# Three moves in the transfer order of a fused attention kernel: q's low parts, the gate load, the attention store

## The chip, the cores and the metric

The kernel runs on one core of a Trainium2 chip. The metric is the device time of one execution in microseconds (us). The engines are named as in the profile: PE (TensorE), DVE (VectorE), ACT (ScalarE), POOL (GpSimd) and SP (SyncE, which here only issues DMAs; ACT issues some too).

## The reference, cut to what matters

A decoder layer on a sequence of 1024 rows of 1024 values, all float32. One normalised input is projected to nine blocks; a convolution branch and an attention branch use them, and a gated merge joins the two. The change lies in the attention branch. It has 24 heads of 64 values, in three groups of eight heads; group g attends in a band at stride 1, 4 or 16. The three groups are then merged by the weights of their softmaxes, and the result is gated by silu of z_att:

```
m = jnp.max(scores, axis=-1)
p = jnp.exp(scores - m[..., None])
den = jnp.sum(p, axis=-1)
o = jnp.einsum('bdhnqk,bdhnke->bdhnqe', p, vb) / den[..., None]
...
m_all = jnp.maximum(jnp.maximum(maxes[0], maxes[1]), maxes[2])
wts = [d_g * jnp.exp(m_g - m_all) for m_g, d_g in zip(maxes, dens)]
w_sum = wts[0] + wts[1] + wts[2]
att = (wts[0][..., None] * outs[0] + wts[1][..., None] * outs[1]
       + wts[2][..., None] * outs[2]) / w_sum[..., None]
y_att = (att * jax.nn.silu(z_att)) @ w_att_out[layer]
```

## The kernel before, in words

**Precision.** Matrices of the projections are split into a high and a low fp32r part, and every product is three matmuls: high by high (L73), low by high (L74), high by low (L75). Of q, too, a high and a low part are kept, so that the scores of one tile are q's high part by k (L843) and its low part by k (L844).

**The attention phase** runs from about 640 to 1082 us as one loop over slots (L970 to L1016). The 24 heads are taken as 12 pairs of heads n, numbered so that n = 3j + g: j is one of four blocks of two heads per group, g the group. A pair has 8 slots, a slot has one unit of work of each kind on PE, in an order that is written out by hand:

1. twelve matmuls L73 to L75 into PSUM tile `d`: the projection of a coming pair's q and k (part 0 and part 1, each in two halves of 512 rows), and after the last pair of the gates;
2. the scores of this slot (L843, L844) into `s`;
3. the transposes (L860) of the exponentials of two slots earlier into `t`, copied to `pt` by DVE (L865) or ACT (L863);
4. the values (L875) of three slots earlier into `o`;
5. what the dictionary `beside` holds for this slot.

DVE masks the scores and takes their maxima (L847, L850), ACT takes the exponentials (L852). The orders of DVE, ACT, POOL and SP are set by a scheduler from the order of the code and its own estimates; each engine then runs its list strictly in that order.

**From projection to scores.** ACT and DVE write each projected part to a tile `kqp` (two buffers; L720, L721). From there small DMAs on SP's queue (`move`, L785, two of 128 KB for each move, eight per part for k and q together) carry k and q to the tiles that PE reads. q's low half goes its own way: `load_low(n)` issues the four `ql` DMAs of pair n in slot 4 of the pair before, together with the load of v (`vt`). DMAs that SP and ACT issue share eight completion semaphores that are handed out in turn, so a DMA is not issued before the one that came eight places earlier in the program has landed; that may be a store of ACT's (`oscr`, L684; `ascr`, L730) which itself still waits for its data.

**The combination.** When the three groups of a block j have stored their outputs to `oscr[j]`, `combine(j, half)` merges them, once for each half of the rows. It is a generator of six steps, and `FIRST` and `SECOND` name the slots, counted from the one in which the last group is done, in which the steps of the two halves are emitted:

- step 1: the load `rd` (L885, 792 KB, one buffer for both halves);
- step 2: maxima (`ma`, L897, L898), differences (L902), an exponential on ACT (L903), and the load `at` of the gate (L905, one buffer for both halves);
- step 3: the small sums and their reciprocal (L908 to L913);
- step 4: two of the three wide products (L917);
- step 5: the third product (L917), two sums (L920, L922), which leave `pr`;
- step 6: four transposes of `pr` on PE (L926) into `t`, the product with the gate (L927), the store to `atscr` (L929).

With n the pair in which block j ends, that slot is 8n + 10. For j = 0, 1, 2 the second half's step 6 falls in the first slot of pairs 5, 8 and 11, that is slots 40, 64 and 88. Slot 40 begins its scores at 844.91 us in the profile, slot 64 at 947.05, slot 88 at 1049.41.

Of the kernel before, what the change touches and what calls it, by code (L numbers as in the profile page):

```python
# [8 lines left out]
F32 = mybir.dt.float32  # L9
# [7 lines left out]
P = 128  # L17
# [22 lines left out]
def layer(ctx: ExitStack, tc: tile.TileContext, a, out):  # L40
    nc = tc.nc
# [10 lines left out]
    def sbuf_pool(name, **kw):  # L52
        return tc.tile_pool(name=name, bufs=1, reuse_waits="tile", **kw)

    def split(hi, lo, raw, lo_eng=None):

        nc.scalar.activation(hi, raw, AF.Copy)  # L57
        (lo_eng or nc.vector).tensor_sub(lo, raw, hi.bitcast(F32))  # L58
# [44 lines left out]
    zascr = [dram.tile([P, S], F32, name=f"zascr{j}") for j in range(4)]  # L103
    atscr = [dram.tile([P, S], F32, name=f"atscr{j}") for j in range(3)]
# [66 lines left out]
    with sbuf_pool("start") as st, tc.manual_schedule(  # L171
# [15 lines left out]
        def load_v(kp):  # L187
            raw = wpool.tile([P, 1024], F32, name="wraw", tag="wraw", bufs=3)
            for c in (slice(0, 512), slice(512, 1024)) if kp == 0 else (slice(0, 1024),):
                nc.sync.dma_start(raw[:, c], a["w_v"][0, kp][:, c])  # L190
            v_raw.append(raw)
# [148 lines left out]
        for kt in range(KT):  # L340
# [10 lines left out]
            for i, (wh, wl) in enumerate(u_w):  # L351
                for half in range(2):
                    s = slice(half * 512, half * 512 + 512)
# [292 lines left out]
    ap_ = c_ctx.enter_context(sbuf_pool("att"))  # L646

    def pair_tile(n, name, dt=F32R):
        return stk.tile([P, 2, S], dt, name=name, tag=f"s{n}")
# [13 lines left out]
    def v_load(vt, g, j):  # L663
        c0 = g * 512 + j * P
        cols = vscr[:, c0:c0 + P]
        if g == 0:
            nc.sync.dma_start(vt, cols.rearrange("(t p) c -> p t c", p=P))
        elif g == 1:
            v = cols.rearrange("(b p r) c -> r p b c", b=2, r=4)
            for r in range(4):  # L670
                nc.sync.dma_start(vt[:, 2 * r:2 * r + 2], v[r])
        else:
            v = cols.rearrange("(i t s) c -> s i t c", t=8, s=2)
            for s in range(2):
                nc.sync.dma_start(vt[64 * s:64 * s + 64], v[s])
# [105 lines left out]
    def move(dst, row, n, part, i, which):  # L781

        for h in range(2):
            src = parts_of[n, part][64 * i + 32 * h:64 * i + 32 * h + 32, which]
            nc.sync.dma_start(dst[row + 32 * part:row + 32 * part + 32, h].bitcast(F32), src.bitcast(F32))  # L785
# [11 lines left out]
    def load_low(n):  # L797

        for part in range(2):
            move(q_low[n % 2], 0, n, part, 1, 1)  # L800
        v2[n] = stk.tile([P, 8, P], F32, name="vt", tag="vt", bufs=2)
        v_load(v2[n], order[n][1], order[n][0])
        if order[n][1] == 0:
            row = ap_.tile([P, 4, P], F32, name="row", tag="pr")
            for i in range(2):
                nc.sync.dma_start(row[:, i], bscr[i:i + 1, order[n][0] * P:(order[n][0] + 1) * P].to_broadcast([P, P]))
            late.append(add_row(v2[n], row))

    def add_row(vt, row):
        nc.vector.tensor_add(row[:, 0], row[:, 0], row[:, 1])  # L810
        yield
        for t in (slice(0, 4), slice(4, 8)):
            nc.vector.tensor_add(vt[:, t], vt[:, t], row[:, 0].unsqueeze(1).to_broadcast([P, 4, P]))
            yield
# [67 lines left out]
    def o_load(j, half):  # L882
        s = slice(half * 512, half * 512 + 512)
        rd = ap_.tile([P, 4, 3, 2, 66], F32, name="rd", tag="rd", bufs=1)
        nc.sync.dma_start(rd.rearrange("p t g h c -> p t (g h c)"),  # L885
                          oscr[j][s].rearrange("(t p) g c -> p t (g c)", p=P))
        return rd

    def combine(j, half):


        s = slice(half * 512, half * 512 + 512)
        rd = o_load(j, half)
        yield
        m, den = rd[:, :, :, :, 65], rd[:, :, :, :, 64]
        ma = ap_.tile([P, 4, 2], F32, name="ma")
        nc.vector.tensor_max(ma, m[:, :, 0], m[:, :, 1])  # L897
        nc.vector.tensor_max(ma, ma, m[:, :, 2])  # L898
        w = ap_.tile([P, 3, 4, 2], F32, name="w")
        wd = ap_.tile([P, 3, 4, 2], F32, name="wd")  # L900
        for g in range(3):
            nc.vector.tensor_sub(w[:, g], m[:, :, g], ma)  # L902
        nc.scalar.activation(w, w, AF.Exp, scale=SCALE)  # L903
        at = ap_.tile([P, 512], F32, name="at")
        nc.sync.dma_start(at, zascr[j][:, s])  # L905
        yield
        for g in range(3):
            nc.vector.tensor_mul(wd[:, g], w[:, g], den[:, :, g])  # L908
        nc.vector.tensor_add(wd[:, 0], wd[:, 0], wd[:, 1])
        nc.vector.tensor_add(wd[:, 0], wd[:, 0], wd[:, 2])  # L910
        nc.vector.reciprocal(wd[:, 1], wd[:, 0])
        for g in range(3):
            nc.vector.tensor_mul(w[:, g], w[:, g], wd[:, 1])  # L913
        yield
        o = [rd[:, :, g, :, 0:64] for g in range(3)]
        for g in range(3):
            nc.vector.tensor_mul(o[g], o[g], w[:, g].unsqueeze(3).to_broadcast([P, 4, 2, 64]))  # L917
            if g == 1:
                yield
        nc.vector.tensor_add(o[0], o[0], o[2])  # L920
        pr = ap_.tile([P, 4, 2, 64], F32, name="pr", tag="pr")
        nc.vector.tensor_add(pr, o[0], o[1])  # L922
        yield
        pt = psa.tile([P, 512], F32, name="t", tag="t")
        for t in range(4):
            nc.tensor.transpose(pt[:, t * P:(t + 1) * P], pr[:, t].rearrange("p h c -> p (h c)"), ident)  # L926
        nc.vector.tensor_mul(at, pt, at)  # L927
        if j < 3:
            nc.sync.dma_start(atscr[j][:, s], at)  # L929
        else:  # L930
            att_parts(3, s, at)
        yield

    ah, al = {}, {}

    def att_parts(j, s, raw):

        if j // 2 not in ah:
            ah[j // 2], al[j // 2] = pair_tile(j // 2, "ah"), pair_tile(2 + j // 2, "al")
        split(ah[j // 2][:, j % 2, s], al[j // 2][:, j % 2, s], raw)  # L940
# [23 lines left out]
    LEAD, TURN, VAL = 13, 2, 3  # L964
    stages = 8 * len(order)

    FIRST, SECOND = (2, 6, 6, 7, 7, 9), (8, 11, 11, 12, 12, 14)
    beside, heads = {}, {}

    with tc.manual_schedule(engines={nc.tensor.engine}):  # L970
        for slot_ in range(-LEAD, (2 * len(order) + KT) * 4 - LEAD):
            due, made[:] = made[:], []
            after = next(stream)
            for x in due:
                move_kq(*x)
                if x == (0, 1):
                    load_low(0)
            if 0 <= slot_ < stages:
                n, st_ = divmod(slot_, 8)
                if st_ == 0:  # L980
                    heads[n] = Attend(n)
                if st_ == 4 and n + 1 < len(order):
                    load_low(n + 1)
                heads[n].scores(st_)
            if TURN <= slot_ < stages + TURN:
                n, st_ = divmod(slot_ - TURN, 8)
                heads[n].turn(st_)
            if VAL <= slot_ < stages + VAL:
                n, st_ = divmod(slot_ - VAL, 8)
                heads[n].values(st_)  # L990
                if st_ == 7:
                    del heads[n]
                    j, g = order[n]
                    if g == 2:
                        for half, steps in enumerate((FIRST, SECOND)):
                            c = combine(j, half)
                            for x in steps:
                                beside.setdefault(slot_ + x, []).append(c)
            for c in beside.pop(slot_, ()):
                next(c)  # L1000
            for c in late:
                for x in (2, 2, 3):
                    beside.setdefault(slot_ + x, []).append(c)
            late[:] = []
            j = slot_ - stages - VAL
            if 0 <= j < 3:
                raw = load_raw(atscr[j])
                for half in range(2):
                    s = slice(half * 512, half * 512 + 512)
                    att_parts(j, s, raw[:, s])  # L1010
            if j in (4, 6, 8):
                w_out(0, j // 2 - 2)
            if j == 11:
                ahead = weights(a["w_ao"][0], 512)
            if after:
                after()  # L1016
        assert not beside and next(stream, None) is None
# [148 lines left out]
```

## Time and profile before

| | |
|---|---|
| time, median of 3 runs | 1278.72 us (1276.84 to 1278.82) |
| the profiled execution | 1277.71 us |
| its span in the trace | 1275.9 us |
| granted clock | 0.999 |
| PE busy | 1248.6 us, 98% |
| DVE, ACT, POOL busy | 890.5, 476.8, 94.7 us |

The profiled execution lies 1.0 us below the median and inside the three runs. Times in the text are microseconds from the start of its span. In rows of the timeline the columns are start, duration, engine, line, operation, tiles, number of instructions, and in brackets the idle time just before and what ended it. In rows of waits they are the total, the number of times and the longest. SPq and ACTq are the queues in which DMAs are issued; the duration there runs from the first issue of a row to the end of the last, waits between them included.

### The profile page before, as it was taken

To read this page: it belongs to the slowest core of one execution; us is meant where nothing else is said; L and a number is where in the kernel's file an instruction comes from. 1 tells how busy PE (TensorE), PEld (TensorE's weight loads), DVE (VectorE), ACT (ScalarE), POOL (GpSimd) and SP (SyncE) were. 2 spreads that over 40 slices of the span, in tenths; PEclk is the share of its full clock that TensorE was granted. 3 is DMA by queue.
4 is the path that set the end of the run, shared out by engine and by line. 5 is a ranking of instruction groups with operands and counts; after the bars stand their busy time and mean duration, and the time that the engine had idled before them with its cause. 6 is when DMAs were issued, how large, how long until landed. Compare 5 with 4: busy or idle time off the path is not lost.

```text
span 1275.9 us, 16604 instructions
## 1 busy us (share of the span) xinstructions
PE 1248.6 (98%) x6148; PEld 1050.6 (82%) x6148; DVE 890.5 (70%) x1576; ACT 476.8 (37%) x911; POOL 94.7 (7%) x78
## 2 busy tenths in 40 slices
PE   6999999999999999999999999999999989999997
PEld 4777888888888888888888888888888878888886
DVE  6777999999999986853345546766766563349544
ACT  4653212111222246720015545545444467534211
POOL 0000000000000000000042111111101012100000
PEclk9999999999999999999999999999999999999999
DMA  9522311211211112545666456576575566659221
GB/s 366 186 95 68 114 60 53 102 50 50 91 58 50 50 52 89 167 164 198 149 171 152 120 130 162 135 198 149 140 206 137 147 166 190 205 176 316 98 100 67
DMA packets 85526, 171.53 MB, mean 134 GB/s; under 512 B 11203, under 2 KB 41027, under 8 KB 85445
## 3 DMA queue, kind: packets, MB, share of 16 engines
q1 hardware_dynamic: 69024, 157.66, 41.9%
q10 hardware_dynamic: 16420, 12.80, 3.3%
q8 instruction: 49, 0.80, 0.3%
q14 instruction: 33, 0.26, 0.1%
HBM read 105.74 MB, written 33.23 MB: 109 GB/s over the span
## 4 chain that ended last, share of the span: by engine, by line
PE 91%; DVE 4%; DMA 2%; ACT 2%; issue 1%; SPq 0%; ACTq 0%; DVEq 0%
PE d L73 22%; PE d L75 22%; PE d L74 22%; PE o L875 4%; PE d L1070 2%; PE d L1069 2%; PE d L467 2%; PE d L466 2%; PE d L1071 2%; PE d L465 2%; PE t L860 2%; PE s L844 1%; PE s L843 1%; PE d L249 1%; PE d L247 1%; PE d L248 1%
## 5 line engine op out<-in xcount | busy, mean ns | idle before, releaser
L73 PE MATMUL d<-hh,whi 128*128 128x512 f32 x1072 | 427.5, 399 | 1.5 <-DVE gs L632 0.9
L74 PE MATMUL d<-hl,whi 128*128 128x512 f32 x1072 | 417.6, 390 | 1.9 <-DVE hl L347 1.9
L75 PE MATMUL d<-hh,wlo 128*128 128x512 f32 x1072 | 418.5, 390 | 0.0
L406 DVE SCALAR_TENSOR_TENSOR v<-u,cw,v 128x1024 f32<-128x1024 f32 x232 | 280.5, 1279 | 0.0
L75 PEld LDWEIGHTS d<-hh,wlo 128*128 128x128 f32 x1072 | 201.2, 188 | 43.9 <-POOL wlo L58 0.7
L74 PEld LDWEIGHTS d<-hl,whi 128*128 128x128 f32 x1072 | 201.7, 188 | 41.7 <-DVE hl L347 2.8
L73 PEld LDWEIGHTS d<-hh,whi 128*128 128x128 f32 x1072 | 201.6, 188 | 40.9 <-ACT whi L57 1.3
L57 ACT ACTIVATE whi<-wraw 128x512 fp32r<-128x512 f32 (+1 forms) x107 | 88.0, 834 | 269.6 <-PE d L74 236.1
L58 POOL TENSOR_TENSOR wlo<-wraw,whi 128x512 fp32r<-128x512 f32 (+1 forms) x56 | 84.8, 1529 | 658.0 <-ACT whi L57 556.2
L852 ACT ACTIVATE sb<-sb,nm 128x128 f32<-128x128 f32 (+1 forms) x192 | 85.0, 444 | 86.9 <-DVE nm L850 82.6
L847 DVE CUSTOM_DVE_ANT_0 sb<-s,mask 128x128 f32<-128x128 f32 (+1 forms) x192 | 59.7, 347 | 61.6 <-PE s L844 54.8
L875 PE MATMUL o<-vt,pt 128*128 128x64 f32 x560 | 73.5, 267 | 1.1 <-ACT pt L863 0.5
L875 PEld LDWEIGHTS o<-vt,pt 128*128 128x128 f32 x560 | 70.1, 192 | 2.1 <-DVE pt L865 1.3
L58 DVE TENSOR_TENSOR wlo<-wraw,whi 128x1024 fp32r<-128x1024 f32 (+1 forms) x51 | 57.9, 1137 | 15.6 <-ACT whi L57 15.0
L844 PE MATMUL s<-k,ql 128*128 128x128 f32 (+1 forms) x192 | 51.0, 279 | 3.2 <-DMA ql<-kqp 3.2
L465 PE MATMUL d<-vh,hh 128*128 128x512 f32 x128 | 49.8, 389 | 0.0
L466 PE MATMUL d<-vl,hh 128*128 128x512 f32 x128 | 49.8, 389 | 0.0
L467 PE MATMUL d<-vh,hl 128*128 128x512 f32 x128 | 49.8, 389 | 0.0
L73 PE MATMUL d<-uh,whi 128*128 128x512 f32 x128 | 49.8, 389 | 0.0
L74 PE MATMUL d<-ul,whi 128*128 128x512 f32 x128 | 49.8, 389 | 0.0
L75 PE MATMUL d<-uh,wlo 128*128 128x512 f32 x128 | 49.8, 389 | 0.0
L632 DVE TENSOR_TENSOR gs<-d,sgc 128x512 f32<-128x512 f32 x16 | 11.1, 691 | 54.9 <-PE d L75 48.8
(224 smaller groups left out, 1758.5 us busy)
## 6 DMA issues: line engine op xcount, KB each, us to landing
wraw<-in_w_t SPq DMA_DIRECT2D x67, 512.0 KB, 4.3
k<-kqp SPq DMA_DIRECT2D x96, 128.0 KB, 2.6
q<-kqp SPq DMA_DIRECT2D x96, 128.0 KB, 2.4
wa<-in_w_ada SPq DMA_DIRECT2D x16, 512.0 KB, 5.9
rd<-oscr SPq DMA_DIRECT2D x8, 792.0 KB, 5.1
ql<-kqp SPq DMA_DIRECT2D x48, 128.0 KB, 2.4
wraw<-in_w_v SPq DMA_DIRECT2D x11, 512.0 KB, 3.6
x<-in_xT SPq DMA_DIRECT2D x8, 512.0 KB, 10.2
```

What stands on the lines that cost most here:

```text
L57: nc.scalar.activation(hi, raw, AF.Copy)
L58: (lo_eng or nc.vector).tensor_sub(lo, raw, hi.bitcast(F32))
L73: nc.tensor.matmul(ps, lh, rh, start=start, stop=False)
L74: nc.tensor.matmul(ps, lh, rl, start=False, stop=False)
L75: nc.tensor.matmul(ps, ll, rh, start=False, stop=stop)
L406: nc.vector.scalar_tensor_tensor(d, u[:, k:k + S], cw[:, ct, k:k + 1], d, op0=mult, op1=add)
L465: nc.tensor.matmul(ps, hh[:, k, ts_], rh, start=k == 0, stop=False)
L466: nc.tensor.matmul(ps, hh[:, k, ts_], rl, start=False, stop=False)
L467: nc.tensor.matmul(ps, hl[:, k, ts_], rh, start=False, stop=k == KT - 1)
L844: nc.tensor.matmul(ps[:, c:c + w], self.ql[:, h, ts_], self.k2[:, h, ks], start=False, stop=True)
L852: nc.scalar.activation(sb[:, c:c + w], sb[:, c:c + w], AF.Exp, bias=nm[:, t - tp:t - tp + 1], scale=SCALE, accum_out=ov[:, t, h, 64:65])
L875: nc.tensor.matmul(self.po[:, t % 4, h], pt[:, c + i:c + i + P], self.vt[:, kb, r], start=i == 0, stop=i + P == w)
```

## The change

Three things are moved.

- `load_low(n)` is cut in two. The `ql` DMAs are issued as soon as part 1 of the pair has been moved, right behind its k and q; `load_v(n)`, the rest, stays in slot 4.
- The load of the gate `at` goes from step 2 to the end of step 5, and the store to `atscr` becomes a step 7, two slots behind step 6. For j = 3 there is no step 7.
- Steps 1 to 6 of the second half are one slot later: `SECOND` was (8, 11, 11, 12, 12, 14) and is (9, 12, 12, 13, 13, 15, 17).

```
+    def load_v(n):
         v2[n] = stk.tile([P, 8, P], F32, name="vt", tag="vt", bufs=2)
         v_load(v2[n], order[n][1], order[n][0])
...
         nc.scalar.activation(w, w, AF.Exp, scale=SCALE)
-        at = ap_.tile([P, 512], F32, name="at")
-        nc.sync.dma_start(at, zascr[j][:, s])
         yield
...
         nc.vector.tensor_add(pr, o[0], o[1])
+        at = ap_.tile([P, 512], F32, name="at")
+        nc.sync.dma_start(at, zascr[j][:, s])
         yield
...
         nc.vector.tensor_mul(at, pt, at)
-        if j < 3:
-            nc.sync.dma_start(atscr[j][:, s], at)
-        else:
+        if j == 3:
             att_parts(3, s, at)
+        yield
+        nc.sync.dma_start(atscr[j][:, s], at)
         yield
...
-    FIRST, SECOND = (2, 6, 6, 7, 7, 9), (8, 11, 11, 12, 12, 14)
+    FIRST, SECOND = (2, 6, 6, 7, 7, 9, 11), (9, 12, 12, 13, 13, 15, 17)
...
                 move_kq(*x)
-                if x == (0, 1):
-                    load_low(0)
+                if x[1]:
+                    load_low(x[0])
+                    if x[0] == 0:
+                        load_v(0)
...
                 if st_ == 4 and n + 1 < len(order):
-                    load_low(n + 1)
+                    load_v(n + 1)
...
-                            for x in steps:
+                            for x in steps[:6 if j == 3 else 7]:
```

Lines of the changed kernel are numbered two higher behind L800 (the load `rd` is L887, the scores' mask L849, the copy of `pt` L867), up to the gate load, which is now L924; the transposes of `pr` are L928, the product L929, the store L933. L922 is the same line in both.

SP's queue is the same in both up to the first combination. There, from the second half of block 0 on, it stood as follows before. `k` and `q` are the DMAs of pair 5, `rd` is the second half of block 0, `wraw` the weights of a later projection, `ql` and `vt` belong to pair 5.

```order
L785 DMA k_5884<-kqp 32x1024 x4
L785 DMA q_5885<-kqp 32x1024 x4
L885 DMA rd<-oscr_4279 128x4x396
L62 DMA wraw<-in_w_t 128x1024 x2
L785 DMA k_5884<-kqp 32x1024 x4
L785 DMA q_5885<-kqp 32x1024 x4
L929 DMA atscr_93<-at 128x512
L785 DMA ql<-kqp 32x1024 x4
L675 DMA vt<-vscr 64x8x128 x2
```

The same place of SP's queue in the changed kernel:

```order
L785 DMA k_5884<-kqp 32x1024 x4
L785 DMA q_5885<-kqp 32x1024 x4
L62 DMA wraw<-in_w_t 128x1024 x2
L785 DMA k_5884<-kqp 32x1024 x4
L785 DMA q_5885<-kqp 32x1024 x4
L785 DMA ql<-kqp 32x1024 x4
L887 DMA rd<-oscr_4279 128x4x396
L675 DMA vt<-vscr 64x8x128 x2
L933 DMA atscr_93<-at 128x512
```

`ql` has come ahead of the store `atscr`, and `rd` has gone behind two weight loads, four k and q transfers and `ql`. The same happens at blocks 1 and 2.

On DVE the second half of block 0 stood in slots 37 to 39 before: `ma` came at once behind L712 of slot 37. In slot 40 DVE's list before read as follows, where `kqp` is the next pair's projection, `sb` the masked scores of slot 41, and `at` the last step of this half.

```order
L865 COPY pt<-t 128x384
L721 TENSOR_TENSOR kqp<-rot,kqp 128x512
L850 TENSOR_SCALAR nm<-ov 128x2
L721 TENSOR_TENSOR kqp<-d,kqp 128x512
L927 TENSOR_TENSOR at<-t,at 128x512
L847 ISA sb,ov<-s,mask_4269 128x128
L847 ISA ov 128x1
```

The same place of DVE's list in the changed kernel:

```order
L867 COPY pt<-t 128x384
L721 TENSOR_TENSOR kqp<-rot,kqp 128x512
L852 TENSOR_SCALAR nm<-ov 128x2
L721 TENSOR_TENSOR kqp<-d,kqp 128x512
L899 TENSOR_TENSOR ma<-rd 128x8
L900 TENSOR_TENSOR ma<-ma,rd 128x8
L904 TENSOR_TENSOR w<-rd,ma 128x8 x3
L908 TENSOR_TENSOR wd<-w,rd 128x8 x3
L909 TENSOR_TENSOR wd<-wd 128x8
L910 TENSOR_TENSOR wd<-wd 128x8
L911 RECIPROCAL wd<-wd 128x8
L913 TENSOR_TENSOR w<-w,wd 128x8 x3
```

The three L917, L920 and L922 follow, with the two masks of slot 41's scores between them. So the whole second half now stands in slots 40 and 41, where before only its last product stood, while PE's transposes of its result have moved by one slot, from 40 to 41. Block 1 has the same rows at slots 64 and 65. At block 2, where no projection of q or k is left, DVE's list in the changed kernel has the chain behind the copy of `pt` of slot 88:

```order
L852 TENSOR_SCALAR nm<-ov 128x2
L867 COPY pt<-t 128x384
L899 TENSOR_TENSOR ma<-rd 128x8
L900 TENSOR_TENSOR ma<-ma,rd 128x8
L904 TENSOR_TENSOR w<-rd,ma 128x8 x3
```

Before, `ma` stood there behind the scores of slot 85. On PE nothing else changes its place than the four transposes of each second half.

## The prediction

> **What bounds the kernel now.** I read the page first, then the waits of PE, then the timelines of PE, SP, DVE and ACT around slots 40, 64 and 88. From the page's first part, and from the waits of PE (total, times, longest) the first two of eight rows and the last:
>
> ```profile
> PE 1248.6 (98%) x6148; PEld 1050.6 (82%) x6148; DVE 890.5 (70%) x1576; ACT 476.8 (37%) x911; POOL 94.7 (7%) x78
> ```
>
> ```profile
> PE d L247 <- ACT wh L235: 11.6, 1, 11.6
> PE s L844 <- DMA ql<-kqp: 3.2, 2, 2.9
> ...
> PE d L249 <- DVE hl L228: 0.4, 1, 0.4
> ```
>
> PE is the bound: 98% busy, and behind the start (11.6) the other seven rows sum to 8.0 us of 1276. The change neither adds nor takes PE work. So it can gain only what PE waits for: 3.2 us for `ql`, at two places, and a little for `pt`. It can lose more, since any transfer or DVE step that comes late for PE is added in full. The question is how much slack the moved pieces had. The places on PE, in slots 40 to 42, 66, and 88 to 90:
>
> ```profile
> 845.42 0.30 PE L844 MATMUL s<-k,ql 128*128 128x128 f32 x1 [0.29 <-DMA ql<-kqp]
> ...
> 846.75 0.61 PE L926 MATMUL t<-ident,pr 128*128 128x128 f32 x4
> 847.11 0.47 PE L73 MATMUL d<-hh,whi 128*128 128x512 f32 x1
> ...
> 851.28 0.48 PE L73 MATMUL d<-hh,whi 128*128 128x512 f32 x1
> ```
>
> ```profile
> 952.96 0.48 PE L73 MATMUL d<-hh,whi 128*128 128x512 f32 x1
> ```
>
> ```profile
> 1052.50 0.30 PE L844 MATMUL s<-k,ql 128*128 128x128 f32 x1 [2.87 <-DMA ql<-kqp]
> ...
> 1058.36 0.48 PE L73 MATMUL d<-hh,whi 128*128 128x512 f32 x1
> ...
> 1062.52 0.88 PE L875 MATMUL o<-vt,pt 128*128 128x64 f32 x6 [0.54 <-ACT pt L863]
> ```
>
> The transposes of `pr` (L926) take 847.11 − 846.75 = 0.36 of PE in slot 40, and will take the same in slot 41. There they stand just ahead of the L73 that opens slot 42's work, at 851.28, 952.96 and 1058.36 in the three blocks.
>
> **Part one: `ql` earlier.** The wait at slot 88 comes from SP's queue. Its rows there, and two of the waits of SP:
>
> ```profile
> 1041.25 0.53 SPq L929 DMA_DIRECT2D atscr<-at  x1
> 1047.29 3.99 SPq L785 DMA_DIRECT2D ql<-kqp  x4
> ```
>
> ```profile
> SPq L785 <- DMA oscr<-ov: 37.8, 14, 6.7
> SPq L785 <- DMA ascr<-gs: 11.6, 2, 6.1
> ```
>
> Issue times and landings of `ql`, from its tile:
>
> ```profile
> L785 SPq DMA_DIRECT2D ql<-kqp x48: 507/589/1745, 668.4 to 1050.7; - x48
> ...
> DMA to landing us min/median/max: 2.2/2.4/4.5
> ```
>
> The first `ql` stood 1047.29 − 1041.78 = 5.5 us behind `atscr`, and the four took 3.99 instead of 4 × 0.59 = 2.4. Both are waits for stores that ACT issues and that share the completion semaphore. The change takes `rd` and `atscr` from ahead of `ql`, so `ql` moves two places in the round of eight: now its third DMA waits for the gate store that its first waited for, till 1047.29. The fourth follows 0.6 later and lands 2.4 behind, at 1050.3. PE asks for it at 1052.50 − 2.87 = 1049.6. So of 2.87 some 0.7 is left; the gain is 2.1 to 2.9, taken as 2.2. At slot 40 the fourth `ql` also waits for a store, of `oscr`; of 0.29 I take 0.2. The 0.54 at 1062.52 is a wait for a copy of ACT's; a PE that is late anyway covers it: 0 to 0.5, taken as 0.4. Gains: **2.8**. For pairs 1 to 4 SP's order is unchanged, so the move is worth nothing there.
>
> **Part two: the second half a slot later and behind `ql`.** `rd` now stands behind the fourth `ql`. The last three `ql` of blocks 0 and 1 got through here:
>
> ```profile
> 842.43 1.77 SPq L785 DMA_DIRECT2D ql<-kqp  x3
> ```
>
> ```profile
> 942.77 2.40 SPq L785 DMA_DIRECT2D ql<-kqp  x3
> ```
>
> And the landings of `rd`, from its tile:
>
> ```profile
> DMA to landing us min/median/max: 4.4/5.1/5.9
> ```
>
> In block 0 three `ql` can go early, the fourth waits for the `oscr` store till 842.4; `rd` follows at 843.0 and lands at 848.1. In block 1 `rd` itself waits for the store that held `ql` till 942.8, and lands at 947.9. In block 2 it goes behind the fourth `ql`, at 1048.4, and lands at 1053.5.
>
> DVE's new list puts `ma` behind its row of slot 40 (64, 88):
>
> ```profile
> 849.08 0.68 DVE L721 TENSOR_TENSOR kqp<-d,kqp 128x512 fp32r<-128x512 f32 x1
> ```
>
> ```profile
> 949.65 0.69 DVE L721 TENSOR_TENSOR kqp<-d,kqp 128x512 fp32r<-128x512 f32 x1
> ```
>
> ```profile
> 1053.68 0.55 DVE L865 COPY pt<-t 128x384 f32<-128x384 f32 x1
> ```
>
> ```profile
> 844.79 0.63 ACT L720 ACTIVATE kqp<-rot 128x512 fp32r<-128x512 f32 x1 [1.58 <-DMA ql<-kqp]
> ```
>
> In block 0 this ends at 849.76, but ACT's L720 ahead of it waited 1.58 for a `kqp` buffer that `ql` was still reading, and the first `ql` now go earlier. So I take 1.3 off: 848.5. In block 1 it ends at 950.3. In block 2 at 1054.2 less the 2.2 gained, 1052.0; there `rd` decides, 1053.5.
>
> From `ma` to `pr`, by rows of blocks 2 and 1, with a mask of a later slot's scores:
>
> ```profile
> 1038.11 0.16 DVE L897 TENSOR_TENSOR ma<-rd 128x8 f32<-128x8 f32 x1
> ...
> 1040.31 2.53 DVE L913 TENSOR_TENSOR w<-w,wd 128x8 f32<-128x8 f32 x3
> ```
>
> ```profile
> 937.11 0.32 DVE L913 TENSOR_TENSOR w<-w,wd 128x8 f32<-128x8 f32 x3
> 937.35 1.89 DVE L917 TENSOR_TENSOR rd<-rd,w 128x512 f32<-128x512 f32 x3
> ...
> 941.82 0.68 DVE L920 TENSOR_TENSOR rd<-rd 128x512 f32<-128x512 f32 x1
> ...
> 943.03 0.68 DVE L922 TENSOR_TENSOR pr<-rd 128x512 f32<-128x512 f32 x1
> ```
>
> ```profile
> 850.54 0.29 DVE L847 CUSTOM_DVE_ANT_0 sb<-s,mask 128x128 f32<-128x128 f32 x1
> ```
>
> 1040.31 − 1038.11 = 2.2 with the exponential on ACT, 937.35 − 937.11 = 0.24, then 1.89 + 0.68 + 0.68, less some 0.15 by which neighbours overlap: 5.55. Two masks of slot 41's scores lie inside it, 0.4 with their overlap. So 5.95, and `pr` is ready at 848.5 + 5.95 = 854.5, at 950.3 + 5.95 = 956.2, at 1053.5 + 5.95 = 1059.5.
>
> PE asks for it in slot 41 at 851.28 − 0.36 − 0.2 = 850.7, at 952.96 − 0.36 = 952.6, and at 1058.36 − 0.36 − 2.2 = 1055.8. Stalls: **3.8, 3.6 and 3.7**, sum 11.1. Before, the same `pr` was ready long ahead:
>
> ```profile
> 839.67 0.68 DVE L922 TENSOR_TENSOR pr<-rd 128x512 f32<-128x512 f32 x1
> ```
>
> 840.35 against 846.75, 6.4 of slack, so nothing of this was on the path.
>
> Bounds. If `rd` landed early everywhere, DVE's order alone leaves 3.8, 3.6, and in block 2 a start at 1052.0, so 2.2: 9.6. I take off up to 2.5 where a free `kqp` lets DVE run sooner than I assumed: 7.1 at the least. At the most `rd` lands in 5.9 (0.8 more in block 2), DVE gains nothing in block 0 (1.3), and an L913 meets a split on POOL, as at 1040.31, where it took 2.53 instead of 0.32 beside this:
>
> ```profile
> 1040.37 2.38 POOL L58 TENSOR_TENSOR wlo<-wraw,whi 128x1024 fp32r<-128x1024 f32 x1 [16.15 <-ACT whi L57]
> ```
>
> 2.2 more: 11.1 + 0.8 + 1.3 + 2.2 = 15.4. Nothing behind the stall is late next: the exponentials of slot 41's scores are turned two slots later, and DVE and ACT catch up while PE stands. Block 3's second half moves by one slot too, with no `rd` behind `ql`: taken as nothing.
>
> **Part three: `at` and `atscr`.** Both are issued a slot or two later. They stand behind `vt` on SP, where no wait of PE's is, and `atscr` is read only behind slot 99. A late gate would hold the product L929 and its `t` buffer, which PE wants two slots, some 8 us, later (851.28 − 847.11 = 4.2 a slot). Value 0. Below nothing it can't go, since PE waits for neither before; at the most 1.0, about what a slow load keeps DVE from its other work.
>
> **Sum.** 11.1 − 2.8 = 8.3 over the profiled execution: 1277.71 + 8.3 = 1286.0. That execution is 1.0 under the median of the runs; on the median the sum gives 1287.0. I state 1286.2, nearer the former, since DVE's start in slot 40 is the softest term and can rather shorten the stalls. Bounds: 7.1 − 3.7 = +3.4 to 15.4 + 1.0 − 2.3 = +14.1.
>
> **The clock.** Stalls of this length may cost once more. At the start, behind 11.6 us of idle PE, matmuls of one shape came every 0.43 us until 17.07, then every 0.24:
>
> ```profile
> 16.64 0.63 PE L247 MATMUL d<-wh,hh 128*128 128x512 f32 x1
> 17.07 0.46 PE L248 MATMUL d<-wl,hh 128*128 128x512 f32 x1
> 17.36 0.40 PE L249 MATMUL d<-wh,hl 128*128 128x512 f32 x1
> 17.60 0.40 PE L247 MATMUL d<-wh,hh 128*128 128x512 f32 x1
> ```
>
> That is some 5.5 us at half pace, worth up to 2.7, though the granted clock reads full. Behind the 2.87 there is no slow stretch: the L73 to L75 of the slot that follows take the usual time. So somewhere between 2.9 and 11.6 us of idle the pace begins to halve. [...]
>
> **The rivals.**
>
> *A. Faster.* The chain stays hidden and only the waits go. This needs `pr` at 850.7, so `ma` at 850.7 − 5.95 = 844.7 and `rd` issued by 839.6, ahead of the store that holds the fourth `ql` till 842.4. Against it, too: `ma` stands behind L721. It decides where the stall is nothing in all three blocks; then 1278.72 − 2.8 = 1275.9. Chance 4%.
>
> *B. No change.* DVE reaches `ma` almost a slot sooner than its rows, the stalls shrink to 1 us each and the gain of 2.8 cancels them: 1278.9. For it speaks that L720 waited for `ql`; against it that `rd` lands only at 848.1 and 947.9. Chance 6%.
>
> *C. Much slower: the pace.* If all three stalls are long enough for the slow stretch, 3 × 2.7 = 8.1 comes on top, 1294; with one, 1289. Chance of 1291 or more 12%.
>
> *D. Milder.* `ql`'s gain is whole and the stalls are near their lower bound: +3.4 to +5, 1282 to 1283. Chance 18%.
>
> **How the numbers follow.** The forecast's own spread, +5 to +12 or so, has the other 60%. The range 1281.0 to 1291.5 takes in D and the forecast and leaves out A, B and most of C. A measurement of this kernel tells 0.2%, 2.6 us, from no change. Faster: A, 0.04. Same: B and a tail of D, 0.07. Slower: 0.89.
>
> **What would show it.** Right: PE's waits list the transposes of `pr` (L928) behind DVE's L922, three times, 3 to 4.5 us each, in slots 41, 65 and 89; `ma` (L899) waits for `rd` in block 2; PE's wait for `ql` falls from 3.2 to about 1; SP issues `rd` near 843, 943 and 1048. Wrong: L928 without a wait, `rd` near its old times, or the 2.9 for `ql` still there. Matmuls at 0.43 us behind a stall would show C.

## The result, and the profile after

The changed kernel takes 1292.05 us (median of 4 runs, 1291.68 to 1293.13), the kernel before 1278.77 beside it: ratio 1.0109, 95% interval 1.0091 to 1.0126. The change costs 13.3 us, half a microsecond more than the range of the prediction held. The profiled execution took 1291.68, its span is 1289.9, and its mean granted clock is 0.992 where it was 0.999.

The waits of PE in the changed kernel, total, times, longest (the first two of seven rows):

```profile
PE t L928 <- DVE nm L852: 12.2, 3, 5.5
PE d L247 <- ACT wh L235: 11.3, 1, 11.3
```

The row for `ql` (3.2 us before) is gone. In its place the transposes of `pr` wait three times for DVE. The view names L852, which stands right behind L922 on DVE; what the transposes need is L922's `pr`. The first of the three places, in the timeline of PE:

```profile
853.66 1.09 PE L928 MATMUL t<-ident,pr 128*128 128x128 f32 x4 [3.34 <-DVE nm L852]
854.40 0.78 PE L73 MATMUL d<-hh,whi 128*128 128x512 f32 x1
854.97 0.63 PE L74 MATMUL d<-hl,whi 128*128 128x512 f32 x1
```

The waits in slots 41, 65 and 89 are 3.34, 3.35 and 5.49 us. And behind each of them the matmuls come every 0.43 us instead of 0.23: half the pace. The windows of the profile around the three waits show why (length, busy time of each engine with its count, then the granted clock, DMA share, GB/s):

```profile
849.90:853.40 3.50, 0.42 (x4) 0.28 (x3) 3.50 (x12) 0.39 (x1) 0.00 (x0) 1.00 1.04 259
853.40:856.80 3.40, 3.14 (x10) 2.69 (x11) 0.19 (x2) 0.88 (x4) 0.00 (x0) 0.50 0.86 265
856.80:860.20 3.40, 3.40 (x23) 3.03 (x22) 0.67 (x2) 1.82 (x4) 1.11 (x1) 1.00 0.00 1
955.80:959.20 3.40, 1.18 (x11) 1.04 (x10) 3.30 (x13) 0.49 (x1) 0.00 (x0) 1.00 0.95 209
959.20:966.00 6.80, 5.67 (x16) 4.64 (x17) 1.06 (x5) 0.88 (x4) 0.00 (x0) 0.50 0.37 119
1064.90:1068.40 3.50, 0.45 (x5) 0.31 (x3) 2.95 (x17) 0.60 (x2) 0.00 (x0) 1.00 1.00 295
1068.40:1075.30 6.90, 4.46 (x13) 3.71 (x14) 3.06 (x10) 1.83 (x5) 2.37 (x1) 0.51 0.57 189
```

At each wait the granted clock falls to 0.50 for one or two stretches of 3.4 us, which begin while PE still waits. The three begin at 853.4, 959.2 and 1068.4, apart by 31 and 32 times 3.41, so they lie on one grid of 3.41 us; a window, below, is a step of this grid.

SP's queue at the three places (`ql`, then `rd`):

```profile
831.96 10.59 SPq L785 DMA_DIRECT2D ql<-kqp  x4
842.60 0.58 SPq L887 DMA_DIRECT2D rd<-oscr  x1
```

```profile
938.34 2.50 SPq L785 DMA_DIRECT2D ql<-kqp  x4
947.13 0.38 SPq L887 DMA_DIRECT2D rd<-oscr  x1
```

```profile
1047.82 10.11 SPq L785 DMA_DIRECT2D ql<-kqp  x4
1057.97 0.59 SPq L887 DMA_DIRECT2D rd<-oscr  x1
```

And DVE's start on the chain in the three blocks, with its end in the first:

```profile
847.82 0.16 DVE L899 TENSOR_TENSOR ma<-rd 128x8 f32<-128x8 f32 x1
...
852.83 0.69 DVE L922 TENSOR_TENSOR pr<-rd 128x512 f32<-128x512 f32 x1
```

```profile
954.48 0.16 DVE L899 TENSOR_TENSOR ma<-rd 128x8 f32<-128x8 f32 x1
```

```profile
1064.99 0.17 DVE L899 TENSOR_TENSOR ma<-rd 128x8 f32<-128x8 f32 x1 [3.46 <-DMA rd<-oscr]
```

In blocks 0 and 1 `ma` waits for no DMA: it starts as soon as DVE's list lets it. In block 2 it waits 3.46 us for `rd`, which took 7.0 us to land, the longest of the `rd` transfers:

```profile
DMA to landing us min/median/max: 4.7/5.4/7.0
```

Where the 14.0 us of the span come from is read from the starts of the scores on PE, slot by slot:

| scores of slot | before | changed | difference |
|---|---|---|---|
| 40 | 844.91 | 844.63 | -0.28 |
| 42 | 854.11 | 858.35 | +4.24 |
| 64 | 947.05 | 951.29 | +4.24 |
| 66 | 955.79 | 966.21 | +10.42 |
| 88 | 1049.41 | 1059.66 | +10.25 |
| 89 | 1057.02 | 1063.83 | +6.81 |
| 90 | 1061.19 | 1076.14 | +14.95 |
| 91 | 1066.24 | 1080.21 | +13.97 |

All of it arises at the three places. Slots 40 to 42 add 4.5, 64 to 66 add 6.2; up to slot 89 3.4 is saved, which is the wait of 2.87 for `ql` and the 0.36 of the transposes that now stand a slot later; slots 89 to 90 add 8.1, and 1.0 comes back by slot 91.

### The profile page after: what moved, and what is told of

Read it like the earlier page. It is cut to its first block, busy times and chain, and to the rows that moved or that the text cites. A ratio compares the mean times of both kernels' runs of the same rounds, so it can differ in the third digit from the quotient of the medians.

```text
span 1289.9 us, 16602 instructions
## 1 busy us (share of the span) xinstructions
PE 1254.4 (97%) x6148; PEld 1055.7 (82%) x6148; DVE 887.7 (69%) x1576; ACT 477.2 (37%) x911; POOL 95.4 (7%) x78
## 4 chain that ended last, share of the span: by engine, by line
PE 90%; DVE 5%; DMA 2%; ACT 2%; issue 1%; SPq 0%; ACTq 0%; DVEq 0%
PE d L73 22%; PE d L75 21%; PE d L74 21%; PE o L877 3%; PE d L1075 2%; PE d L1074 2%; PE d L466 2%; PE d L465 2%; PE d L1073 2%; PE d L467 2%; PE t L862 2%; PE s L846 1%; DMA rd<-oscr 1%; PE s L845 1%; PE d L249 1%; PE d L247 1%
## 5 line engine op out<-in xcount | busy, mean ns | idle before, releaser
L849 DVE CUSTOM_DVE_ANT_0 sb<-s,mask 128x128 f32<-128x128 f32 (+1 forms) x192 | 60.0, 347 | 71.0 <-PE s L846 67.1
## 6 DMA issues: line engine op xcount, KB each, us to landing
x<-in_xT SPq DMA_DIRECT2D x8, 512.0 KB, 10.2
```

## The experiments

My theory after the result: the second half's chain comes late for PE because `rd` is placed behind `ql`, in SP's queue and in the scheduler's eyes, and each wait of PE brings a stretch at half clock, which costs more on top. The rivals are that one move alone does it, that the late gate has a share, or that the half clock has another cause. The ratios are to runs of the kernel before on the same chip. In short:

| run | median us | ratio, 95% interval |
|---|---|---|
| first move alone | 1280.05 | 1.0013, 1.0003 to 1.0022 |
| third move alone | 1284.98 | 1.0052, 1.0037 to 1.0067 |
| first and third | 1297.90 | 1.0154, 1.0137 to 1.0171 |
| first and second | 1278.36 | 1.0002, 0.9992 to 1.0011 |
| changed, stalls filled | 1286.63 | 1.0065, 1.0050 to 1.0080 |
| changed, stalls half filled | 1286.63 | 1.0059, 1.0044 to 1.0074 |
| changed, transposes later | 1280.64 | 1.0014, 1.0005 to 1.0024 |
| before, `ql` on POOL's queue | 1270.45 | 0.9939, 0.9922 to 0.9956 |
| changed, step 1 back | 1277.63 | 0.9990, 0.9980 to 0.9999 |
| changed, `ql` on POOL's queue | 1270.41 | 0.9938, 0.9921 to 0.9955 |
| before, its stall filled | 1277.78 | 0.9995, 0.9986 to 1.0004 |

### One: `ql` early, alone

```
-                if x == (0, 1):
-                    load_low(0)
+                if x[1]:
+                    load_low(x[0])
+                    if x[0] == 0:
+                        load_v(0)
...
-                    load_low(n + 1)
+                    load_v(n + 1)
```

> Before with only the first move: ql issued right behind k and q. DVE's list has the second half where it was before. Theory (the stalls need the shift of the second half together with the early ql): no wait of the transposes of pr, the two waits for ql (3.2 us) gone, 1275.5 us, that is 0.2 to 0.3% under before. Rival (the early ql by itself pushes the loads rd late): a wait of the transposes of 3 us or more in slots 40, 64 and 88 and 1285 or more.

Neither came true: no wait of the transposes, but no gain either. PE's waits:

```profile
PE d L75 <- POOL wlo L58: 1.7, 1, 1.7
PE s L846 <- DMA ql<-kqp: 1.3, 1, 1.3
PE d L73 <- ACT whi L57: 1.0, 1, 1.0
```

At slot 88 1.3 of the wait for `ql` is left. I put it down to stores of ACT's that its later DMAs wait for: in the changed kernel, which has the same move, the third waits 7.7 us for `ascr` there. By slot 90 PE meets weights of the gates that are late. The two waits together are 2.7 us, 2.1 of them inside one window, and a half-clock stretch follows:

```profile
1062.00:1065.40 3.40, 1.28 (x4) 0.78 (x5) 0.00 (x0) 3.37 (x6) 2.96 (x2) 1.00 0.47 151
1065.40:1068.80 3.40, 3.40 (x9) 2.63 (x8) 0.00 (x0) 2.85 (x7) 1.72 (x1) 0.50 0.83 274
```

So what is saved at slot 88 is given back at slot 90: the wait for `ql` had covered a later one.

### Two: the second half later, alone

```
-    FIRST, SECOND = (2, 6, 6, 7, 7, 9), (8, 11, 11, 12, 12, 14)
+    FIRST, SECOND = (2, 6, 6, 7, 7, 9), (9, 12, 12, 13, 13, 15)
```

> Before with only the third move: the second half's steps one slot later, ql and the gate as before. DVE's list now has ma behind the maxima of slot 39's scores, ahead of slot 40's L721. Theory (shift and early ql are needed together): no wait of the transposes of 1 us or more, the 2.9 us for ql at slot 88 stays, some small waits behind DVE's projection steps in slot 41; 1278 to 1281 us. Rival (the shift alone makes the stalls): three waits of 3 us or more and a granted clock under 0.995; 1290 or more.

It costs 6.4 us, which lies between the two expectations, though the transposes wait for nothing. The waits of PE:

```profile
PE d L73 <- DVE rot L710: 6.0, 5, 2.7
```

Two of the five are 2.69 us, in slots 41 and 65. DVE has the chain ahead of slot 40's L721 and L710, and L710 reads the `d` that PE wants to use again: PE waits not for the chain but for what stands behind it. Both are followed by a half-clock stretch of 3.4 us, here the first:

```profile
846.90:850.30 3.40, 1.41 (x6) 1.19 (x7) 3.40 (x10) 0.62 (x1) 0.00 (x0) 1.00 0.41 93
850.30:853.70 3.40, 3.40 (x12) 2.77 (x11) 1.38 (x4) 0.89 (x5) 0.00 (x0) 0.51 0.62 136
```

Thus the shift alone is about half of the loss, and it does not need the early `ql`: `rd` goes out at 833.01 here, ahead of `ql`, and the `pr` of block 0 is ready at 848.2. In slot 40 DVE has no room for the chain, whichever side of L721 it stands on.

### Three: the first and the third move together

The edits of the two runs above, without the gate's.

> Before with the first and the third move, the gate's load and store as before. DVE's list is that of the changed kernel at slot 40: ma behind L721. Theory: this is the whole effect, three waits of the transposes of 3.3, 3.3 and 4 to 5.5 us, granted clock 0.99, 1290 to 1293 us. Rival (the late gate and store are part of the cost): 1284 or less, with waits of 2 us or less.

```profile
PE t L928 <- DVE pr L924: 16.9, 3, 8.0
```

The loss is there, and it is dearer than I expected, 1297.90 (the profiled execution took 1294.97): the waits are 5.60, 3.29 and 8.04. Up to `ma` DVE's list in slot 40 is that of the changed kernel. On SP `rd` now also stands behind the store `atscr`. In block 0 it is issued no later than in the changed kernel, at 842.32, but lands 7.7 us later where it took 5.0 there, and `ma` waits for it; why it takes longer isn't shown:

```profile
850.02 0.17 DVE L899 TENSOR_TENSOR ma<-rd 128x8 f32<-128x8 f32 x1 [2.21 <-DMA rd<-oscr]
```

So the second move takes some 6 us off in the changed kernel (1297.90 - 1292.05, which were not timed beside each other); it is no part of the cost.

### Four: the first and the second move together

```
-    FIRST, SECOND = (2, 6, 6, 7, 7, 9, 11), (9, 12, 12, 13, 13, 15, 17)
+    FIRST, SECOND = (2, 6, 6, 7, 7, 9, 11), (8, 11, 11, 12, 12, 14, 16)
```

> The changed kernel with the second half back in its old slots (8, 11, 11, 12, 12, 14, store at 16): first and second move together. Theory: no wait of the transposes, no wait for ql, 1275.5 us, the same as the first move alone. Rival (the late gate and store cost by themselves): 1279 or more, with a wait of PE for a buffer t or of DVE for the gate in front of it.

```profile
PE t L862 <- ACT pt L865: 2.3, 1, 2.3
...
PE s L846 <- DMA ql<-kqp: 1.2, 1, 1.2
```

The three waits and the half-clock stretches of slots 41, 65 and 89 are gone, which is what the run was for. The gain of 3 us isn't there. In the profiled execution, which at 1276.83 is one of the fastest of ten (the slowest, 1280.85, has a granted clock of 0.995), 1.2 for `ql` is left, and 2.3 for a copy of ACT's at slot 90 takes the place of 0.5. ACT is held there by a weight:

```profile
1059.14 1.06 ACT L57 ACTIVATE whi<-wraw 128x1024 fp32r<-128x1024 f32 x1 [6.46 <-DMA wraw<-in_w_t]
```

### Five and six: PE kept busy through the stalls

```
         pt = psa.tile([P, 512], F32, name="t", tag="t")
+        for i in range((14, 14, 23, 0)[j] * half):
+            nc.tensor.matmul(pt, hh[:, i % KT, 0:P], hh[:, i % KT, 0:512], start=True, stop=True)
```

> The changed kernel, and in front of the transposes of pr of the second halves of blocks 0, 1 and 2 PE does 14, 14 and 23 extra matmuls (128x512, 0.23 us each) into the tile that the transposes then overwrite; they ask for nothing that is late. PE reaches the transposes as early or late as pr does, so the stalls become busy time. Theory (each stall is followed by a stretch at half the granted clock because PE stood idle, some 6.3 us in all): clock 0.999, no half-clock stretch, 1285.8 us, 6 under the changed kernel. Rival (the half-clock stretches come from something else in these slots): clock 0.992 and 1292 us.

The extra matmuls are work for nothing, and the kernel is 5.4 us shorter by the medians (1292.05 and 1286.63, which were not timed beside each other). The same windows as above show no half clock:

```profile
849.90:853.40 3.50, 3.50 (x19) 2.84 (x18) 3.50 (x12) 0.48 (x1) 0.00 (x0) 1.00 1.02 234
853.40:856.80 3.40, 3.40 (x18) 2.69 (x17) 0.27 (x2) 0.88 (x4) 0.00 (x0) 1.00 0.69 228
955.80:959.20 3.40, 3.40 (x18) 2.54 (x17) 3.03 (x10) 0.33 (x2) 0.00 (x0) 1.00 0.92 227
959.20:966.00 6.80, 6.80 (x39) 5.83 (x38) 2.12 (x7) 3.28 (x11) 2.54 (x2) 1.00 0.38 94
```

DVE and SP run the same lists, but for the product with the gate, which stands two places earlier on DVE in two blocks, and one load of the gate on SP. At slot 91 this kernel is 7.8 us behind the kernel before (1074.03 against 1066.24), the changed one 14.0. The difference, 6.2, is the price of the half clock. The theory holds, its rival falls.

The next run has 7, 7 and 16 of these matmuls instead of 14, 14 and 23.

> As the run before, with 7, 7 and 16 extra matmuls, so that some 1.7 us of idle PE is left ahead of the transposes at each place. Theory with a threshold near 1.9 us of idle in one window of 3.4: no half-clock stretch, 1285.8 us, the same as with the stall filled. Rival (any idle of over 1 us may do it): half-clock stretches at one or more of the three places and 1287 to 1292 us.

Its time is that of the full filling. The waits left in slots 41 and 65 are 1.57 each, without a half-clock stretch. But at slot 88 a wait of 1.55, for `ql`, has one:

```profile
1055.50:1058.90 3.40, 1.85 (x15) 1.61 (x14) 0.90 (x6) 2.07 (x3) 0.00 (x0) 1.00 0.79 194
1058.90:1062.30 3.40, 3.40 (x9) 2.63 (x8) 0.86 (x6) 0.69 (x4) 0.00 (x0) 0.50 1.10 318
```

So 1.9 us of idle, just under the least that stood ahead of half clock until then (3.40 - 1.41 = 1.99 in run two), is no threshold: here 3.40 - 1.85 = 1.55 was enough. And the run speaks for neither side cleanly: waits of the same length differ. The four executions differ too, from 1284.27 to 1286.94.

### Seven: the transposes two slots later

```
-    FIRST, SECOND = (2, 6, 6, 7, 7, 9, 11), (9, 12, 12, 13, 13, 15, 17)
+    FIRST, SECOND = (2, 6, 6, 7, 7, 9, 11), (9, 12, 12, 13, 13, 17, 19)
+    THIRD = (9, 12, 12, 13, 13, 15)
...
-                        for half, steps in enumerate((FIRST, SECOND)):
+                        for half, steps in enumerate((FIRST, SECOND if j < 3 else THIRD)):
```

> The changed kernel with the transposes of pr of the second halves of blocks 0, 1 and 2 two slots later (17 instead of 15, the store at 19), slots 43, 67 and 91. The order of DVE and SP up to there is as in the changed kernel. Theory (PE only asked too early): the three waits gone, clock 0.999, 1275 to 1278 us. Rival (the late chain holds something else, a buffer t or the weights, that PE meets later): new waits of 3 us or more and 1281 or more.

```profile
PE d L73 <- ACT whi L57: 2.7, 1, 2.7
PE d L75 <- POOL wlo L58: 1.6, 1, 1.6
```

The waits of the transposes are gone, so PE did only ask too early. The time, 1280.64, lies between the two expectations: at slot 90 the gates' weights are late again, 2.7 and 1.6, with a half-clock stretch of 6.8 us, from 1061.2 to 1068.0.

### Eight: `ql` on POOL's queue

```
-    def move(dst, row, n, part, i, which):
+    def move(dst, row, n, part, i, which, eng=nc.sync):
...
-            nc.sync.dma_start(dst[row + 32 * part:row + 32 * part + 32, h].bitcast(F32), src.bitcast(F32))
+            eng.dma_start(dst[row + 32 * part:row + 32 * part + 32, h].bitcast(F32), src.bitcast(F32))
...
-            move(q_low[n % 2], 0, n, part, 1, 1)
+            move(q_low[n % 2], 0, n, part, 1, 1, nc.gpsimd)
```

> Before, with the ql DMAs issued from POOL's queue instead of SP's, at the same place of the program; nothing else moved. They then share no completion semaphore with stores of ACT's and stand behind no atscr. Theory (the 3.2 us for ql are waits of SP's queue): the waits for ql gone, 1275 to 1276 us unless the freed slots let a late weight take its place, then 1277. Rival (POOL's own queue, behind its splits, is as late): waits for ql of 3 us or more, 1279 or more.

The kernel before with this edit takes 1270.45 us, 8.7 less, far more than the 3 us that the theory gave it, and beats both kernels. PE's waits, all rows:

```profile
PE d L247 <- ACT wh L235: 11.5, 1, 11.5
PE d L74 <- DVE hl L347: 1.8, 2, 1.1
PE d L73 <- DVE gs L632: 0.9, 1, 0.9
PE d L249 <- DVE hl L228: 0.4, 1, 0.4
PE o L875 <- DVE pt L865: 0.2, 1, 0.2
```

Nothing is left of `ql`, `rot` and nearly nothing of `pt`: the attention phase has no wait of 0.4 us or more. `ql` is not faster on this queue, it lands later:

```profile
DMA to landing us min/median/max: 2.9/4.3/7.6
```

What is gained, as I read it, is that 48 transfers no longer stand in SP's queue behind stores of ACT's, nor hold up the weights behind them. By the slots, the span's 7.5 us are 0.7 at slot 0, another 2.8 spread from slot 25 to 88, 3.0 at slot 89 and 1.0 at slot 91. The last two are waits of the list of before. The spread ones are too small for it, and I have not traced them.

### Nine: one number back

```
-    FIRST, SECOND = (2, 6, 6, 7, 7, 9, 11), (9, 12, 12, 13, 13, 15, 17)
+    FIRST, SECOND = (2, 6, 6, 7, 7, 9, 11), (8, 12, 12, 13, 13, 15, 17)
```

> The changed kernel with one number changed: step 1 of the second half, the load rd, back at slot 8 (before: 8, changed: 9); steps 2 to 7 stay at 12, 12, 13, 13, 15, 17. rd then stands on SP ahead of the weight loads, and the scheduler puts ma on DVE behind L712 of slot 37 again. Theory (the late place of rd behind ql, in the scheduler's eyes too, is what puts the chain into slot 40): no wait of the transposes, 1276 to 1279 us, clock 0.997 or more. Rival (the later steps 2 to 5 put it there): waits of 3 us at three places and 1288 or more.

```profile
824.89 0.36 SPq L887 DMA_DIRECT2D rd<-oscr  x1
825.36 0.92 SPq L62 DMA_DIRECT2D wraw<-in_w_t  x2
```

1277.63 us: the loss is gone. With step 1 one slot earlier, all else as in the changed kernel, SP issues `rd` at 824.89 instead of 842.60, and the scheduler moves the whole chain back to slots 37 to 39 although its steps are still emitted in slots 38 and 39. The rival falls.

### Ten: the change with `ql` on POOL's queue

The edit of run eight in the changed kernel.

> The changed kernel with the ql DMAs issued from POOL's queue, nothing else moved. ql no longer stands ahead of rd on SP, and shares no semaphore with ACT's stores; DVE's list has ma in slot 38 to 39. Theory (the change's loss needs ql in front of rd on SP's queue): no wait of the transposes of 1 us or more, 1270 to 1275 us. Rival (the shifted second half is late anyway): waits of the transposes of 3 us or more, 1280 or more.

```profile
827.73 0.57 SPq L887 DMA_DIRECT2D rd<-oscr  x1
```

1270.41, as fast as run eight. All three moves are in, and none costs anything: `rd` goes out at 827.73, ahead of what held it, `ma` of block 0 starts at 839.00, and `pr` is ready at 846.1, 3.0 before PE turns it at 849.14. In the runs at hand the shift hurts where `rd` stands on SP behind transfers that wait for stores of ACT's: behind `ql` in the changed kernel, behind `k` in run two.

### Eleven: the stall of the kernel before filled

Twelve matmuls as in run five, in the kernel before, ahead of the scores of slot 88.

> Before, with 12 extra matmuls (128x512, 2.8 us) on PE ahead of the scores of slot 88, where it otherwise waits 2.9 us for ql; nothing else moved. Theory (the wait of 2.9 is long enough for a half-clock stretch in some executions of the kernel before, though not in the profiled one): the median falls by 1 to 2 us, to 1277, and the spread of its executions narrows. Rival (no execution of before has one there): the same time as before, 1278.5 to 1279.5, and the same spread.

By the time it is undecided: 1277.78 against 1278.81, and the interval holds 1. The spread is 2.4 us against 3.6. The granted clocks say more. Of the 15 executions of the kernel before that were timed beside this run, 13 have 0.996 or 0.997 and two have 0.999; of the 11 with the stall filled, ten have 0.998 or 0.999 and one has 0.997. A mean lower by 0.003 is an estimated 7.7 us at half clock (0.003 of 1276 us is lost, and half clock loses one half). So most executions of the kernel before seem to hold a half-clock stretch that the profiled one, at 0.999, doesn't show, and filling slot 88 takes most of it away. Only one execution of each is profiled, so the place isn't shown directly.

## Why the prediction was wrong

The direction and the places were right, the size was not: +8.3 was forecast and +14.0 measured on the profiled execution, 1292.05 against a range that ended at 1291.5.

**Where the steps held.** `rd` was put at 843.0, 942.8 and 1048.4 on before's scale. With PE's delay at that place it came at 842.6, at 947.1 (942.8 + 4.2 = 947.0) and at 1058.0 (1048.4 + 10.2 = 1058.6). `ma` was put at 848.5 and 950.3; it came at 847.8 and 954.5 (950.3 + 4.2). The chain took 853.52 - 847.82 = 5.70 where I had 5.95. The stalls 3.8 and 3.6 came out as 3.34 and 3.35. The round of eight held: in each of the two traces the 605 transfers of SP and ACT count on eight semaphores, 75 or 76 on each, and in block 2 it is the third `ql` that waits for ACT's gate store (7.7 us for `ascr`).

**Two terms were off in size and cancelled in part.** Block 2's stall was 5.49 and not 3.7. `rd` took 7.0 to land where I took the median of 5.1 (bound 5.9); two transfers of `vt`, the store `atscr` and one of weights were issued meanwhile. Of these 1.9, 0.9 came back, since `rd` was issued 0.6 earlier than forecast and the chain was 0.25 shorter. The other 0.7 of the difference is `ql`'s: its gain was the whole 3.2, not 2.4, so PE asked for `pr` that much earlier. Stalls less gains: 12.2 - 3.2 - 0.5 = 8.5, beside a forecast of 8.3. Run five, the changed kernel without the half clock, gives 7.8 to 8.4 by the two ways of counting, its span (1284.3 - 1275.9 = 8.4) and its slot 91.

**The step that failed is the one on the clock.** It named what comes, matmuls at 0.43 us behind a stall, and left its price out of the sum: 1291 or more got a chance of 12%. That this would be rare was my estimate alone, and no run bears it out: all three stalls, of 3.34, 3.35 and 5.49 us, were followed by half clock, one for one window and two for two. The price is 853.66 to 858.35, 4.69 us, for the work that took 3.19 before (846.75 to 849.94), so 1.5; in slot 65 it is 2.7, in slot 89 2.1: 6.3 together, where run five saves 6.2. With this term the sum of 8.3 would have been 14.6, beside the 14.0 measured. (The upper bound of the sum, +14.1, holds 14.0 only by luck: it is made of a later `rd`, a later DVE and a split on POOL, not of the clock.) In the traces the window ahead of half clock isn't always idle: PE was busy for 0.42 of 3.50 us in one, but 1.18 of 3.40 in another, 1.41 and 1.28 in runs two and one, and 1.85 in run six. A window with PE half busy (1.85 of 3.40) can be enough, and both stalls of 2.69 in run two were followed by half clock.

The other half of this step was to read the quiet 2.87 us of slot 88 as a bound. In the changed kernel the half clock at the end of the span begins at 1286.9, 127 times 3.413 us behind the one at 853.4, so there the grid held that long. In the kernel before it begins at 1273.3, at its end. Counted back by 65 times 3.413 us, an edge lies at an estimated 1051.4, inside the wait (1049.6 to 1052.5):

```profile
1048.00:1051.40 3.40, 1.64 (x8) 1.13 (x6) 0.00 (x0) 3.23 (x7) 0.00 (x0) 1.00 0.73 170
1051.40:1054.80 3.40, 2.30 (x19) 2.25 (x20) 1.14 (x6) 2.17 (x5) 0.00 (x0) 1.00 0.95 230
1269.90:1273.30 3.40, 0.00 (x0) 0.00 (x0) 2.38 (x9) 0.20 (x1) 0.00 (x0) 1.00 0.08 32
1273.30:1275.90 2.60, 0.00 (x0) 0.00 (x0) 0.00 (x0) 0.00 (x0) 0.00 (x0) 0.50 0.43 160
```

By this estimate 1.8 us of the wait fell in one window and 1.1 in the next; neither was followed by half clock. It was a single case, and the grid doesn't lie the same in every execution: at block 0 the half clock begins at 853.4 in the changed kernel, at 853.0 in run three and at 850.4 in run two, where a step back from 853.4 would be 850.0. A wait can fall on it in another way the next time, so a single case bounds nothing. It was also a rare one: of the 60 executions of the kernel before that were timed beside the eleven runs, 8 have the granted clock of the profiled one, 0.999, with a median of 1276.9 us; the other 52 have 0.996 or 0.997, with a median of 1278.9. Nor does PE's busy time alone tell the windows apart: 1.64 of 3.40 here, in eight matmuls, seven of them 512 columns wide, was not followed by half clock, and 1.85 in run six, in fifteen mostly narrower ones, was. What tells them apart isn't shown.

**The rivals.** A named a condition, `rd` issued before 839.6 and `ma` started by 844.7, that keeps the transposes from waiting, as runs two, nine and ten show. It isn't enough by itself: in run two (`rd` at 833.01, `ma` at 841.98) PE waited instead for what stood behind the chain on DVE. B didn't come: no stall shrank to 1 us. C is what happened, in a milder form than its three times 2.7.

**The gain of 2.8** that the prediction booked for the early `ql` is real only inside the changed kernel, where PE is late anyhow. By itself it is given back two slots later (runs one and four), which the prediction didn't see.

## What to carry to other kernels

Ask of every transfer what it is put behind, and count the queue's waits in front of that: `rd` moved by one slot in the code and by 17.7 us on SP (824.89 in run nine, 842.60 in the changed kernel), since it fell behind four transfers that wait for another engine's stores. Where PE is the bound, a stall can cost more than its length: it can bring one or two windows of 3.4 us at half clock, which cost 1.5 to 2.7 us here. Stalls of 1.55 (run six) and 2.69 us (run two) brought one, others of 1.57 (run six), 2.33 (run four) and 2.87 us (the kernel before) did not, so which of them will is not known beforehand. And a queue that is shared by transfers in a hurry and transfers that must wait is relieved by moving the few in a hurry to a queue that is nearly idle, even if they land later there: in run eight POOL takes 0.49 us for each `ql`, they land in 4.3 us instead of 2.4, and the kernel is 8.7 us shorter.

## What was not expected of the hardware

- The granted clock falls to 0.50 on a grid of 3.41 us. In the attention phase it stayed there for one window (runs one, two and six, block 0 of the changed kernel) or two (its blocks 1 and 2, block 0 of run three, and run seven), where PE stood still for 1.1 to 2.9 us of the next window too; in block 2 of run three, with a wait of 8.04 us, it stayed for three. Matmuls that serve nothing but to keep PE busy make the kernel 5.4 us shorter.
- At the start of the trace of the kernel before the matmuls run at the slow pace for 5.5 us behind 11.6 us of idle PE, and yet the granted clock reads 1.00 there. The trace's first record of the clock begins at 17.2 us, just where the pace doubles, so the column doesn't show that stretch.
- Transfers issued from POOL (run eight) take 0.49 us of POOL each and land in a median of 4.3 us, from SP (the kernel before) in 2.4 (`ql`, 128 KB).
